# Layer norms of a two-layer encoder step: variance and scale on whole rows instead of token columns and diagonals

## The chip, the cores and the metric

The kernel runs on one core of one Trainium2 chip. The metric is the device time of one execution in microseconds, from runs of the whole program. The engines are named as the profile names them: PE (TensorE, matrix products), PEld (its weight loads), DVE (VectorE), ACT (ScalarE), POOL (GpSimd) and SP (SyncE, which issues the DMAs). Each engine takes its instructions in the order in which the program was written; a wait on a semaphore holds up all that stands behind it on that engine.

## The reference

One inference step of an encoder with two layers, on 576 tokens (512 of a new prompt and 64 of a running stream) of 1024 features. Layer 0 mixes with an mLSTM and a retention in parallel, layer 1 with multi-head latent attention. After each mixer and after each SwiGLU feed-forward network (FFN) stands a residual addition and a layer norm:

```python
def layer_norm(x, g, b):
    mu = mean(x); var = mean(square(x - mu))
    return (x - mu) * rsqrt(var + LN_EPS) * g + b

for layer in range(2):
    m = mixer_ab(x, ...) if layer % 2 == 0 else mixer_c(x, ...)      # each ends in "@ w_out"
    x = layer_norm(ALPHA * x + m, ln_mix_g[layer], ln_mix_b[layer])
    x = layer_norm(ALPHA * x + (silu(x @ w_g) * (x @ w_u)) @ w_down, ln_ffn_g[layer], ln_ffn_b[layer])

def mixer_c(x, ...):
    cq, ckv, kr = split(x @ w_in, (512, 256, 64))
    cq, ckv = rms_norm(cq, g_q), rms_norm(ckv, g_kv)
    q = cq @ w_uq; k, v = ckv_all @ w_ukv      # 8 heads, 128 + 64 rotary columns
    o = softmax(mask(q k^T)) v                 # block-causal, chunks of 64
    return o @ w_out, ckv, rope(kr)
```

All inputs and outputs are float32.

## The kernel before

The activations lie with features on the 128 partitions and tokens along the free dimension: `Z` holds eight feature tiles m = 0 to 7 of 576 tokens. A float32 product is made from a rounded high and a low part of each operand (`Xh`, `Xl`, and for a weight tile `raw` the pair of tiles `r` that ACT casts at line 364 and DVE splits at line 362), three passes of PE for each product. A weight is split shortly before PE uses it.

The tokens are worked in two halves, 288 and 288 around a mixer's output and 320 and 256 around an FFN. So there are eight layer norms: after the mixer of layer 0 (number 0), after its FFN (1), after the attention (2) and after the last FFN (3), each for half 0 and half 1. While half 0 is being normed, PE works on half 1's last output tiles; while half 1 is being normed, PE begins the next stage with half 0.

The steps of one norm are these. For each feature tile m PE leaves the product in a PSUM bank of the pool `mm`, which has three banks, and DVE adds it to the residual in `Z` (the feed, `ln_feed`, lines 1185 and 1187). That addition is also what frees the bank: the tile three places later in the ring can't begin until it is done. `ln_sums` adds the tile to a running sum `s1` (line 1226, DVE), squares it on ACT (line 1223) and adds the square to `s2` (line 1233, DVE). After m = 7 `ln_finish` reduces `s1` and `s2` over the partitions on PE, works out the variance and its inverse root, and then goes over the tiles: `mean` (line 1265, DVE) subtracts the mean, `scaled` (line 1279, DVE) multiplies by gain and inverse root, ACT adds the bias and rounds (lines 1311 and 1318, `Xh` and `Z`), POOL (line 1319) or DVE (line 1314) makes `Xl`. The PSUM banks of these reductions come from a second pool, `x`, with four banks; a single further bank, `o`, collects an attention head's output.

Before the change the inverse root is worked on token columns: PE turns each 128 tokens of `s1` and `s2` into a column by a product with the constant `cvec`, DVE makes ten small operations on 128x3 numbers (lines 1254 to 1256 and `rsqrt`, 539 to 543), puts the three columns on the diagonals of three 128x128 tiles (line 1261), and PE multiplies these by `ones`, which spreads the roots over a row again in the bank R.

The order of the work is written out by hand. Long steps are generators; `spawn` sets one to go on at a later time of a clock that counts PE's modelled time, and `tick`, called between products, lets the due ones run. The pauses are the table `LAG`: `l1` ahead of `ln_finish`, and `l2` in its middle, between the small operations and the scaling of the tiles. What comes due later is written later into each engine's queue.

Behind norm 1 stands the attention's input projection. For its queries (`cq`, two 512-column products of tokens, then a key/value product `kv` of 320 columns) a norm of its own is made for each block of 128 tokens (`norm`, lines 1730 on ACT and 1731 to 1733 on DVE, again with `rsqrt`). In the attention a head's first block, the sample's 64 tokens, has a second accumulator in columns 64 to 128 of the bank `o`; ACT copies the first (line 2021) and DVE adds it (line 2022), the bank addition.

Of the kernel before, what the change touches and what calls it, by code (L numbers as in the profile page):

```python
# [217 lines left out]
class Kern:  # L218
# [335 lines left out]
    def setup(self):  # L554
# [359 lines left out]
    def retention(self):  # L914
# [16 lines left out]
        def s2(i):  # L931
# [30 lines left out]
            ve, hv, tt, rs = (self.smalls(4) for _ in range(4))  # L962
# [68 lines left out]
    def mlstm(self, h, done):  # L1031
# [43 lines left out]
        def s3(half):  # L1075
            ts = HTILES[half]
            n, i0 = len(ts), ts[0]
            den, rc, ve, hv, tt, rs = (self.smalls(n) for _ in range(6))
# [16 lines left out]
            self.rsqrt(rs, ve, hv, tt)  # L1095
# [119 lines left out]
    def ln_sums(self, s, m):  # L1215
        nc = self.nc
        z = self.zt(s.half, m, s.cut)
        if m == 0:
# [7 lines left out]
        nc.vector.tensor_tensor(s.s1, s.first if m == 1 else s.s1, z, ALU.add)
# [9 lines left out]
    def ln_finish(self, s):  # L1236
# [3 lines left out]
        sl = [(0, 128, 0), (128, 256, 0)]  # L1240
        if n > 256:
            sl.append((n - 128, n, 384 - n))
        J = len(sl)
# [9 lines left out]
        dl, vv, hv, tt, rs = (self.smalls(J) for _ in range(5))  # L1253
        V.tensor_copy(dl, x3[:, 0, :, 0])
# [30 lines left out]
        if tail:  # L1285
            A.copy(s.s2, R[:, 0:n])
            A.copy(s.cb, xd[:, 0:n])
            for m in (6, 7):
                z = self.zt(s.half, m, s.cut)
                G.tensor_tensor(z, z, s.cb, ALU.subtract)  # L1290
                G.tensor_tensor(z, z, s.s2, ALU.mult)
            zs = [scaled(m) for m in range(3)]
# [2 lines left out]
            V.tensor_scalar(zs[4], zs[4], bias(4), None, ALU.add)
# [376 lines left out]
    def layer1(self):  # L1672
# [54 lines left out]
        def norm(i, ps, n, g, y):  # L1727
            L = TLEN[i]
            ss, ve, hv, tt, rs = (self.smalls(1)[0:L] for _ in range(5))
            A.activation(y[0:L, 0:n], ps[0:L, 0:n], AF.Square, accum_out=ss)  # L1730
            V.tensor_scalar(ve, ss, 1.0 / n, RMS_EPS, ALU.mult, ALU.add)
# [224 lines left out]
        def attn(h):  # L1956
# [48 lines left out]
            def sc(i):  # L2005
# [7 lines left out]
                if i == 0:  # L2013
# [8 lines left out]
                    V.tensor_tensor(x[:, 64:128], x[:, 64:128], tmp, ALU.add)
# [240 lines left out]
```

## Time and profile before

| | us |
|---|---|
| three runs | 1393.73, 1391.89, 1393.08 (median 1393.08) |
| the profiled execution, its own time | 1393.54 |
| its span, first to last instruction | 1391.6 |
| PE busy | 1351.7 (97%), 9759 instructions |
| DVE busy | 979.5 (70%), 2277 |
| ACT busy | 610.8 (44%), 1295 |
| POOL busy | 155.0 (11%), 182 |
| mean granted TensorE clock | 0.992 |

All the rows below come from one profiled execution of this kernel. A row of the timeline has a group's start, its length until the last of it ended, the engine, the line, the operation, output and inputs, the shape, how many there are, and in brackets the idle time of the engine just ahead with what ended it. A row of the waits has the total, how often, and the longest.

### The profile page before, as it was taken

Reading aid. Unit: us, or ns where it says so; the run is one execution under the profiler, and the core shown is the slowest. Engines: PE = TensorE matmul, PEld = TensorE weight load, DVE = VectorE, ACT = ScalarE, POOL = GpSimd, SP = SyncE. Lnnn points to the kernel's source line nnn. Section 1 sums busy time; section 2 is a strip of 40 time slices with the busy share of each in tenths; the row PEclk is TensorE's granted clock in tenths of the full one; section 3 lists DMA queues with packets and bytes.
Section 4 is the critical chain, followed back from the end, with each engine's and each line's share of the span. In section 5 each row is a group of like instructions: output and inputs, shape, how many; then the busy total and the mean of one; then the engine's idle time right before and its main releaser. Section 6 shows DMA issues by size and latency. Waiting matters only on the chain.

```text
span 1391.6 us, 24628 instructions
## 1 busy us (share of the span) xinstructions
PE 1351.7 (97%) x9759; PEld 1305.6 (94%) x9759; DVE 979.5 (70%) x2277; ACT 610.8 (44%) x1295; POOL 155.0 (11%) x182
## 2 busy tenths in 40 slices
PE   8999999999999999999999999999999999999995
PEld 6778999999999999999987899999999999999995
DVE  6757677678873685588898565667888358647876
ACT  4422333445551453255354466543555235425533
POOL 1100001115000000000021533311320000000000
PEclk9999999999999999999999999999999999999997
DMA  6121122611232123223321000021213312222221
GB/s 218 61 61 55 47 75 59 194 60 61 88 108 79 62 103 109 76 92 95 117 86 59 31 31 31 32 92 44 94 61 108 106 61 92 91 91 77 93 75 68
DMA packets 38234, 112.91 MB, mean 81 GB/s; under 512 B 5024, under 2 KB 12512, under 8 KB 38120
## 3 DMA queue, kind: packets, MB, share of 16 engines
q1 hardware_dynamic: 38120, 111.35, 24.3%
q8 instruction: 76, 1.25, 0.4%
q14 instruction: 38, 0.31, 0.1%
HBM read 107.45 MB, written 3.89 MB: 80 GB/s over the span
## 4 chain that ended last, share of the span: by engine, by line
PE 83%; DVE 10%; ACT 3%; DMA 2%; issue 2%; POOL 0%; SPq 0%; POOLq 0%; ACTq 0%; DVEq 0%
PE mm L465 44%; PE x L465 36%; PE x L533 2%; DVE r L362 2%; DVE Z L1279 1%; DMA raw<-in_w 1%; DVE Z L1265 1%; PE o L465 1%; ACT Xh L1311 1%; DMA Z<-in_x 1%; ACT r L364 0%; ACT Z L1318 0%; DVE small L542 0%; DVE small L541 0%; DVE small L543 0%
## 5 line engine op out<-in xcount | busy, mean ns | idle before, releaser
L465 PE MATMUL mm<-H,r 128*128 128x320 f32 (+2 forms) x2832 | 387.6, 297 | 0.0
L465 PEld LDWEIGHTS mm<-H,r 128*128 128x128 f32 x2832 | 378.3, 189 | 0.3
L465 PE MATMUL x<-Xh,r 128*128 128x288 f32 x1216 | 244.7, 296 | 0.0
L465 PE MATMUL mm<-Xh,r 128*128 128x288 f32 (+2 forms) x1152 | 229.2, 297 | 6.4 <-DVE Z L1185 2.8
L364 ACT CAST r<-raw 128x512 fp32r<-128x512 f32 (+2 forms) x292 | 178.0, 646 | 104.6 <-PE mm L465 76.0
L362 DVE TENSOR_TENSOR r<-raw,r 128x512 fp32r<-128x512 f32 (+2 forms) x276 | 194.4, 733 | 38.0 <-ACT r L364 37.8
L465 PE MATMUL x<-r,r 128*128 128x288 f32 (+2 forms) x1534 | 211.7, 293 | 0.2 <-DVE r L1055 0.2
L465 PEld LDWEIGHTS x<-r,r 128*128 128x128 f32 x1534 | 205.9, 188 | 0.5 <-DVE r L1055 0.5
L465 PEld LDWEIGHTS x<-Xh,r 128*128 128x128 f32 x1216 | 194.6, 188 | 0.5
L465 PEld LDWEIGHTS mm<-Xh,r 128*128 128x128 f32 x1152 | 183.4, 189 | 7.7 <-ACT Z L1318 3.8
L465 PE MATMUL x<-Xl,r 128*128 128x288 f32 x608 | 179.5, 295 | 0.0
L465 PE MATMUL mm<-Xl,r 128*128 128x288 f32 (+2 forms) x576 | 167.1, 298 | 0.0
L364 ACT CAST r<-T 128x512 fp32r<-128x512 f32 (+1 forms) x114 | 86.9, 762 | 127.5 <-DVE T L397 112.0
L465 PEld LDWEIGHTS x<-Xl,r 128*128 128x128 f32 x608 | 114.1, 188 | 0.0
L362 DVE TENSOR_TENSOR r<-T,r 128x512 fp32r<-128x512 f32 (+1 forms) x114 | 96.3, 866 | 18.6 <-ACT r L364 18.6
L465 PEld LDWEIGHTS mm<-Xl,r 128*128 128x128 f32 x576 | 107.2, 189 | 0.1
L465 PE MATMUL mm<-r,Xh 128*128 128x512 f32 (+1 forms) x320 | 98.8, 391 | 4.6 <-DVE r L699 2.6
L1319 POOL TENSOR_TENSOR Xl<-Z,Xh 128x288 fp32r<-128x288 f32 (+2 forms) x36 | 30.7, 853 | 467.0 <-ACT Z L1318 466.5
L465 PEld LDWEIGHTS mm<-r,Xh 128*128 128x128 f32 x320 | 58.8, 192 | 17.9 <-issue 3.0
L1223 ACT ACTIVATE T<-Z 128x288 f32<-128x288 f32 (+2 forms) x56 | 24.8, 443 | 91.8 <-DVE Z L1185 47.4
L465 PE MATMUL mm<-r,Xl 128*128 128x512 f32 (+1 forms) x160 | 61.3, 383 | 0.0
L1580 DVE TENSOR_TENSOR T<-T,x 128x288 f32<-128x288 f32 x38 | 17.2, 453 | 59.1 <-PE x L465 59.1
(316 smaller groups left out, 1725.9 us busy)
## 6 DMA issues: line engine op xcount, KB each, us to landing
raw<-in_w SPq DMA_DIRECT2D x169, 512.0 KB, 3.5
r<-in_w SPq DMA_DIRECT2D x20, 512.0 KB, 3.4
Z<-in_x SPq DMA_DIRECT2D x1, 1280.0 KB
o_y<-Z SPq DMA_DIRECT2D x2, 640.0 KB, 3.3
Z<-in_x SPq DMA_DIRECT2D x2, 512.0 KB, 7.2
Z<-in_x SPq DMA_DIRECT2D x1, 1024.0 KB, 8.7
o_y<-Z SPq DMA_DIRECT2D x4, 256.0 KB, 2.1
Z<-in_x SPq DMA_DIRECT2D x3, 320.0 KB, 4.9
```

The source lines that it names most:

```text
L362: self.lo_engine.tensor_tensor(t[:, 1], src, t[:, 0].bitcast(F32), ALU.subtract)
L364: self.nc.scalar.copy(t[:, 0], src)
L465: self.nc.tensor.matmul(out, lhsT, rhs, start=start, stop=stop, skip_group_check=more)
L533: self.nc.tensor.transpose(out, in_, self.ident[0:n, 0:n])
L1223: nc.scalar.activation(q, z, AF.Square)
L1265: V.tensor_tensor(z, z, xd[:, 0:n], ALU.subtract)
L1279: V.scalar_tensor_tensor(z, z, gain(m), R[:, 0:n], ALU.mult, ALU.mult)
L1311: A.activation(self.Xh[:, a:b], z, AF.Identity, bias=bias(m))
L1319: G.tensor_tensor(self.Xl[:, a:b], z, self.Xh[:, a:b].bitcast(F32), ALU.subtract)
L1580: V.tensor_tensor(s[:, 0:n], s[:, 0:n], ps, ALU.add)
```

## The change

It has four parts.

1. The norm's middle. The `cvec` products, the small operations on token columns, the diagonals and the later `ones` products are gone. PE makes two full-row products, `ones` with `s1` into the bank `xd` (the mean in every partition) and `ones` with `s2` into R; ACT squares `xd`; DVE works out variance and inverse root on whole rows of 288, 320 or 256 numbers, with `rsqrt` writing its last result into R.
2. The pause `l2` is 1.5 for all eight norms (3 to 7 before).
3. The tail, norm 3 of half 1: the last additions to `s1` and `s2` are left out, and PE adds tile 7 and its square to the two banks by two more products. The order of the last tiles among DVE, POOL and ACT is a new one.
4. In the attention, the bank addition of the sample's block moves from right behind its own products to just ahead of the rounding that reads the bank.

```diff
 LAG = {...
-       "l200": 4.5, "l201": 4.5, "l210": 3, "l211": 7, "l220": 3, "l221": 3, "l230": 4.5, "l231": 4.5, "lc2": 0.3,
+       "l200": 1.5, "l201": 1.5, "l210": 1.5, "l211": 1.5, "l220": 1.5, "l221": 1.5, "l230": 1.5, "l231": 1.5, "lc2": 0.3,
...
-    def rsqrt(self, y, v, hv, t):
+    def rsqrt(self, y, v, out, t):
         V.tensor_scalar(y.bitcast(I32), v.bitcast(I32), -0.5, float(0x5F1FFFF9), ALU.mult, ALU.add)
-        for a, b in ((-0.703952253, 0.703952253 * 2.38924456), (-0.50000016, 1.50000048)):
+        for a, b, to in ((-0.703952253, 0.703952253 * 2.38924456, y), (-0.50000016, 1.50000048, out)):
             V.tensor_tensor(t, y, y, ALU.mult)
             V.scalar_tensor_tensor(t, t, a, v, ALU.mult, ALU.mult)
-            V.scalar_tensor_tensor(y, t, b, y, ALU.add, ALU.mult)
+            V.scalar_tensor_tensor(to, t, b, y, ALU.add, ALU.mult)
... ln_sums
+        if m == 7 and s.last and s.half:
+            return
         nc.vector.tensor_tensor(s.s1, s.first if m == 1 else s.s1, z, ALU.add)
... ln_finish
-        for q, src in enumerate((s.s1, s.s2)):
-            for j, (a, b, _) in enumerate(sl):
-                self.mm(x3[:, q, j, :], src[:, a:b], self.cvec[:, 0:2], True, True)
-            if q == 0:
-                self.mm(xd[:, 0:n], self.ones, s.s1, True, True)
-        V.tensor_copy(dl, x3[:, 0, :, 0])
-        V.scalar_tensor_tensor(vv, dl, -1.0, dl, ALU.mult, ALU.mult)
-        V.scalar_tensor_tensor(vv, x3[:, 1, :, 0], LN_EPS, vv, ALU.add, ALU.add)
-        self.rsqrt(rs, vv, hv, tt)
-        for j in range(J):
-            V.tensor_scalar(d, self.ident, rs[:, j:j + 1], 1024.0, ALU.mult, ALU.mult)
+        self.mm(xd[:, 0:n], self.ones, s.s1, True, not tail)
+        if not tail:
+            self.mm(R[:, 0:n], self.ones, s.s2, True, True)
+        else:
+            self.mm(R[:, 0:n], self.ones, s.s2, True, False)
+            self.mm(xd[:, 0:n], self.ones, self.zt(s.half, 7, s.cut), False, True)
+            self.mm(R[:, 0:n], self.ones, s.q, False, True)
+        t, v, y = R[:, 0:n], s.cb, s.s1
...
-        for m in range(lnv if tail else 2):
-            mean(m)
+        A.activation(v, xd[:, 0:n], AF.Square)
+        mean(0)
+        if tail:
+            c = self.tmp("h", n)
+            A.copy(c, xd[:, 0:n])
+            for m in (6, 7, 5):
+                G.tensor_tensor(z, z, c, ALU.subtract)
+        V.scalar_tensor_tensor(v, t, LN_EPS, v, ALU.add, ALU.subtract)
+        self.rsqrt(y, v, t, t)
+        mean(1)
         yield LAG[f"l2{s.which}{s.half}"]
-        R = self.xbank()
-        for (a, b, c), d in zip(sl, dg):
-            self.mm(R[:, a + c:b], self.ones, d[:, c:128], True, True)
... the tail
-            A.copy(s.cb, xd[:, 0:n])
             for m in (6, 7):
-                G.tensor_tensor(z, z, s.cb, ALU.subtract)
                 G.tensor_tensor(z, z, s.s2, ALU.mult)
-            zs = [scaled(m) for m in range(3)]
...
+            for m in range(6):
+                if m in (2, 3, 4):
+                    mean(m)
+                z = scaled(m)
+                if m in (1, 3):
+                    V.tensor_scalar(z, z, bias(m), None, ALU.add)
-            for m in (0, 6, 7, 2, 3, 5):
+            for m in (0, 2, 6, 4, 5, 7):
... the attention
-                    tmp = self.smalls(64)
-                    A.copy(tmp, x[:, 0:64])
-                    V.tensor_tensor(x[:, 64:128], x[:, 64:128], tmp, ALU.add)
                     return
...
+                    if not half:
+                        tmp = self.smalls(64)
+                        A.copy(tmp, x[:, 0:64])
+                        V.tensor_tensor(x[:, 64:128], x[:, 64:128], tmp, ALU.add)
                     split(self.Xh[:, a:b], self.Xl[:, a:b], x[:, c:c + b - a])
```

The other callers of `rsqrt` give their result as `out` and work as before. In the changed file the lines have other numbers: the feed is at 1176 and 1178, `mean` at 1247, `scaled` at 1267, `Xl` at 1302, the norm of the queries at 1719 to 1721, the bank addition at 2029.

The shorter pause moves instructions in DVE's queue. The first place is norm 1, half 0. Here `mm_7121` (before) and `mm_7101` (after) are the banks with half 1's tile m = 4. Before, on DVE:

```order
L1265 TENSOR_TENSOR Z_69<-Z_69,x_7072 128x320
L1279 SCALAR_TENSOR_TENSOR Z_69<-Z_69,lnv_79,x_7134 128x320
L1265 TENSOR_TENSOR Z_69<-Z_69,x_7072 128x320
L1279 SCALAR_TENSOR_TENSOR Z_69<-Z_69,lnv_79,x_7134 128x320
L1187 TENSOR_TENSOR Z_69<-Z_69,mm_7121 128x256
L1233 TENSOR_TENSOR T_3_71<-T_3_71,T_2_70 128x256
L1226 TENSOR_TENSOR T_3_71<-T_3_71,Z_69 128x256
L1265 TENSOR_TENSOR Z_69<-Z_69,x_7072 128x320
L1279 SCALAR_TENSOR_TENSOR Z_69<-Z_69,lnv_79,x_7134 128x320
```

Four of the eight scalings stood behind the feed of m = 4. After, on DVE, from the sixth scaling on:

```order
L1267 SCALAR_TENSOR_TENSOR Z_69<-Z_69,lnv_78,x_7043 128x320
L1247 TENSOR_TENSOR Z_69<-Z_69,x_7042 128x320
L1267 SCALAR_TENSOR_TENSOR Z_69<-Z_69,lnv_78,x_7043 128x320
L1247 TENSOR_TENSOR Z_69<-Z_69,x_7042 128x320
L1267 SCALAR_TENSOR_TENSOR Z_69<-Z_69,lnv_78,x_7043 128x320
L1178 TENSOR_TENSOR Z_69<-Z_69,mm_7101 128x256
L1226 TENSOR_TENSOR T_3_71<-T_3_71,T_2_70 128x256
L1219 TENSOR_TENSOR T_3_71<-T_3_71,Z_69 128x256
```

Now all eight stand ahead of it. In norm 0 the order changes in the same way, there with two more pairs of weight splits of line 362 between.

The second place is norm 1, half 1, in the queue of DVE beside the projection of the queries; `r_389`, `r_392` (before) and `r_389`, `r_394` (after) are split weights of the key/value product. Before:

```order
L362 TENSOR_TENSOR r_389_6753<-raw_417_7243,r_389_6753 128x320
L362 TENSOR_TENSOR r_392_6787<-raw_417_7243,r_392_6787 128x320
L1731 TENSOR_SCALAR small_75<-small_75 128x1
L539 TENSOR_SCALAR small_75<-small_75 128x1
L541 TENSOR_TENSOR small_75<-small_75 128x1
L542 SCALAR_TENSOR_TENSOR small_75<-small_75 128x1
L543 SCALAR_TENSOR_TENSOR small_75<-small_75 128x1
L541 TENSOR_TENSOR small_75<-small_75 128x1
L542 SCALAR_TENSOR_TENSOR small_75<-small_75 128x1
L543 SCALAR_TENSOR_TENSOR small_75<-small_75 128x1
L1733 SCALAR_TENSOR_TENSOR T_2_70<-mm_7277,small_75,T_2_70 128x512
L362 TENSOR_TENSOR r_392_6787<-raw_417_7243,r_392_6787 128x320
```

After it stood two more splits, two more norms of this kind and only then the eight scalings of half 1. Now, behind the first five splits:

```order
L1267 SCALAR_TENSOR_TENSOR Z_69<-Z_69,lnv_78,x_7270 128x256 x2
L1247 TENSOR_TENSOR Z_69<-Z_69,x_7269 128x256
L1267 SCALAR_TENSOR_TENSOR Z_69<-Z_69,lnv_78,x_7270 128x256
L1247 TENSOR_TENSOR Z_69<-Z_69,x_7269 128x256
L1267 SCALAR_TENSOR_TENSOR Z_69<-Z_69,lnv_78,x_7270 128x256
L1719 TENSOR_SCALAR small_75<-small_75 128x1
L539 TENSOR_SCALAR small_75<-small_75 128x1
L541 TENSOR_TENSOR small_75<-small_75 128x1
```

Four scalings stand ahead of the first of the queries' norms and of the three last splits, and the other four ahead of the second norm. ACT's queue moves with it: four `Xh` of line 1299 stand ahead of the square sum of that norm (line 1718) and of the three casts.

The third place is the attention's first head on DVE (`o_8200` and `o_8149` are the bank o, line 1902 or 1890 prepares keys). Before:

```order
L1984 TENSOR_SCALAR T_2_70<-T_2_70,small_75 128x512
L1902 SCALAR_TENSOR_TENSOR T_434_7596<-mm_8147,T_434_7596 128x256
L2022 TENSOR_TENSOR o_8200<-o_8200,small_75 128x64
L1938 SCALAR_TENSOR_TENSOR T_434_7596<-x_8209,T_434_7596 64x320
L1938 SCALAR_TENSOR_TENSOR T_434_7596<-x_8215,T_434_7596 64x256
L1898 TENSOR_TENSOR Xl_73<-o_8200,Xh_72 128x320
```

After:

```order
L1972 TENSOR_SCALAR T_2_70<-T_2_70,small_75 128x512
L1890 SCALAR_TENSOR_TENSOR T_429_7545<-mm_8096,T_429_7545 128x256
L1926 SCALAR_TENSOR_TENSOR T_429_7545<-x_8156,T_429_7545 64x320
L1926 SCALAR_TENSOR_TENSOR T_429_7545<-x_8162,T_429_7545 64x256
L2029 TENSOR_TENSOR o_8149<-o_8149,small_75 128x64
L1886 TENSOR_TENSOR Xl_73<-o_8149,Xh_72 128x320
```

The addition now stands right ahead of the operation that reads its result, behind all of the head's products into the bank.

More of the change, by code (lines that the diff above doesn't have):

```diff
@@ L961, in s2 @@
             mv = self.smalls(8).rearrange("p (h c) -> p h c", h=4)
-            ve, hv, tt, rs = (self.smalls(4) for _ in range(4))
+            ve, tt, rs = (self.smalls(4) for _ in range(3))
             for h in range(4):
@@ L1077, in s3 @@
             n, i0 = len(ts), ts[0]
-            den, rc, ve, hv, tt, rs = (self.smalls(n) for _ in range(6))
+            den, rc, ve, tt, rs = (self.smalls(n) for _ in range(5))
             bs = self.smalls(6 * n).rearrange("p (i c) -> p i c", i=n)
@@ L1239, in ln_finish @@
         n = s.n
[L1240 to L1243, printed above, removed]
         tail = s.last and s.half
-        lnv = 6 if tail else KT
-        x, xd = self.xbank(), self.xbank()
-        x3 = x[:, 0:4 * J].rearrange("p (q j c) -> p q j c", q=2, j=J)
-        for q, src in enumerate((s.s1, s.s2)):
-            for j, (a, b, _) in enumerate(sl):
-                self.mm(x3[:, q, j, :], src[:, a:b], self.cvec[:, 0:2], True, True)
-            if q == 0:
-                self.mm(xd[:, 0:n], self.ones, s.s1, True, True)
-        dl, vv, hv, tt, rs = (self.smalls(J) for _ in range(5))
-        V.tensor_copy(dl, x3[:, 0, :, 0])
-        V.scalar_tensor_tensor(vv, dl, -1.0, dl, ALU.mult, ALU.mult)
-        V.scalar_tensor_tensor(vv, x3[:, 1, :, 0], LN_EPS, vv, ALU.add, ALU.add)
-        self.rsqrt(rs, vv, hv, tt)
-        dg = []
-        for j in range(J):
-            d = self.diag()
-            V.tensor_scalar(d, self.ident, rs[:, j:j + 1], 1024.0, ALU.mult, ALU.mult)
-            dg.append(d)
+        xd, R = self.xbank(), self.xbank()
+        self.mm(xd[:, 0:n], self.ones, s.s1, True, not tail)
[6 more added lines that the diff above has]
+        t, v, y = R[:, 0:n], s.cb, s.s1
         def mean(m):
@@ L1265, in mean @@
             V.tensor_tensor(z, z, xd[:, 0:n], ALU.subtract)
-        for m in range(lnv if tail else 2):
-            mean(m)
+        A.activation(v, xd[:, 0:n], AF.Square)
[4 more added lines that the diff above has]
+            for m in (6, 7, 5):
+                z = self.zt(s.half, m, s.cut)
+                G.tensor_tensor(z, z, c, ALU.subtract)
+        V.scalar_tensor_tensor(v, t, LN_EPS, v, ALU.add, ALU.subtract)
+        self.rsqrt(y, v, t, t)
+        mean(1)
         yield LAG[f"l2{s.which}{s.half}"]
-        R = self.xbank()
-        for (a, b, c), d in zip(sl, dg):
-            self.mm(R[:, a + c:b], self.ones, d[:, c:128], True, True)
         w = s.which
@@ L1286, in ln_finish @@
             A.copy(s.s2, R[:, 0:n])
-            A.copy(s.cb, xd[:, 0:n])
             for m in (6, 7):
                 z = self.zt(s.half, m, s.cut)
-                G.tensor_tensor(z, z, s.cb, ALU.subtract)
                 G.tensor_tensor(z, z, s.s2, ALU.mult)
-            zs = [scaled(m) for m in range(3)]
-            V.tensor_scalar(zs[1], zs[1], bias(1), None, ALU.add)
-            zs += [scaled(m) for m in range(3, 6)]
-            V.tensor_scalar(zs[4], zs[4], bias(4), None, ALU.add)
-            for m in (0, 6, 7, 2, 3, 5):
+            for m in range(6):
[5 more added lines that the diff above has]
+            for m in (0, 2, 6, 4, 5, 7):
                 z = self.zt(s.half, m, s.cut)
                 A.activation(z, z, AF.Identity, bias=bias(m), scale=gain(m) if m > 5 else 1.0)
-                if m in (0, 7, 3, 5):
+                if m in (0, 2, 5, 7):
                     store(m - m % 2, m - m % 2 + 1)
@@ L1728, in norm @@
             L = TLEN[i]
-            ss, ve, hv, tt, rs = (self.smalls(1)[0:L] for _ in range(5))
+            ss, ve, tt, rs = (self.smalls(1)[0:L] for _ in range(4))
             A.activation(y[0:L, 0:n], ps[0:L, 0:n], AF.Square, accum_out=ss)
             V.tensor_scalar(ve, ss, 1.0 / n, RMS_EPS, ALU.mult, ALU.add)
-            self.rsqrt(rs, ve, hv, tt)
+            self.rsqrt(rs, ve, rs, tt)
             V.scalar_tensor_tensor(y[0:L, 0:n], ps[0:L, 0:n], rs, g[0:L], ALU.mult, ALU.mult)
```

12 lines of the change are left out of this document (2 added, 10 removed).

## The prediction

> **What bounds the kernel now.** I read the page's busy times first, then PE's waits by what ended them, and then the timeline around each norm.
>
> ```profile
> PE 1351.7 (97%) x9759; PEld 1305.6 (94%) x9759; DVE 979.5 (70%) x2277; ACT 610.8 (44%) x1295; POOL 155.0 (11%) x182
> PE o L465 <- DVE o L2022: 3.9, 5, 1.1
> ```
>
> PE works 97% of the span, so a microsecond taken off PE counts wherever PE isn't already waiting. The largest sum of waits by cause is the bank addition that the change moves (3.9 in five waits, the longest 1.1). Nearly all of the other waits that the change can touch lie at the norms, and the rows below show DVE or ACT ending them. So two questions decide: does PE still wait at the norms, and is DVE's queue later or earlier there?
>
> **Part 1, PE's own work.** At norm 0, half 0:
>
> ```profile
> 287.99 0.72 PE L465 MATMUL x<-cvec,T 128*128 128x2 f32 x6
> 288.57 0.73 PE L465 MATMUL x<-T,ones 128*128 128x288 f32 x2
> 289.14 0.73 PE L465 MATMUL x<-cvec,T 128*128 128x2 f32 x6
> 296.14 0.75 PE L465 MATMUL x<-T,ones 128*128 128x128 f32 x6
> 309.11 2.37 PE L465 MATMUL mm<-Xh,r 128*128 128x288 f32 x16 [2.66 <-ACT Z L1318]
> 334.01 0.53 PE L465 MATMUL mm<-Xh,r 128*128 128x288 f32 x2 [0.82 <-ACT Xh L1311]
> ```
>
> From start to start the full row costs 0.57 and each set of columns about 0.58; the spreading of the roots takes another 0.59. The change leaves two full rows, 1.14 in place of 2.33, so PE is relieved of 1.19 a norm, some 7 us over all eight, with less for the narrower ones. But in both halves PE waits afterwards (2.66 and 0.82): there the saving only lengthens the wait, unless what PE waits for comes earlier too.
>
> **Part 1, DVE's chain.** The same norm on DVE, and three rows of ACT:
>
> ```profile
> 289.90 0.16 DVE L1254 COPY small<-x 128x3 f32<-128x3 f32 x1 [0.52 <-PE x L465]
> 292.48 0.81 DVE L1265 TENSOR_TENSOR Z<-Z,x 128x288 f32<-128x288 f32 x2
> 294.74 2.50 DVE L362 TENSOR_TENSOR r<-raw,r 128x512 fp32r<-128x512 f32 x4 [0.34 <-ACT r L364]
> 297.16 0.45 DVE L1185 SCALAR_TENSOR_TENSOR Z<-Z,mm 128x288 f32<-128x288 f32 x1
> 299.11 0.45 DVE L1265 TENSOR_TENSOR Z<-Z,x 128x288 f32<-128x288 f32 x1
> 299.59 0.52 DVE L1279 SCALAR_TENSOR_TENSOR Z<-Z,lnv,x 128x288 f32<-128x288 f32 x1
> 308.52 0.45 DVE L1185 SCALAR_TENSOR_TENSOR Z<-Z,mm 128x288 f32<-128x288 f32 x1
> 294.10 2.17 ACT L364 CAST r<-raw 128x512 fp32r<-128x512 f32 x4
> 308.45 0.54 ACT L1318 ACTIVATE Z<-Z,lnv 128x288 f32<-128x288 f32 x1
> 309.45 0.54 ACT L1318 ACTIVATE Z<-Z,lnv 128x288 f32<-128x288 f32 x1
> ```
>
> From the copy to the end of the second mean it takes 3.4 (289.90 to 293.29). A full-row operation that needs the one before costs 0.48 (299.11 to 299.59). The new middle has eight such steps and two means of about 0.4: 4.6, and ahead of it one square on ACT. No row shows these operations at full width in this place; I take 0.48, the nearest row; the ends are 0.40 (the pair of means is 0.81) and 0.55. The chain is 1.2 longer, but starts 0.25 earlier, since it needs one product and a square of 0.45 instead of three sets. So DVE is about 1.0 later at each norm, in exchange for no round trip over PE.
>
> **Part 2, the shorter pause.** This is where I expect the time to go. Half 1's tile m = 7 uses the bank of m = 4, and may not start until DVE has fed m = 4. Before, that feed stood amid the scalings (297.16). Now it stands behind all eight. In norm 0: second mean at 294.25, feed of m = 3 (three operations, 1.1) to 295.35, four scalings 2.75 to 298.1; then four splits, for which ACT casts (2.17) only after its four pairs of `Xh` and `Z`, 1.0 each (308.45 to 309.45), so to 302.0 and the last split to 302.6; four more pairs 3.65 to 306.25; the feed to 306.6. PE, which before took 3.23 a tile (five tiles and the spreading from 289.72 to 306.45), is ready for m = 7 at 302.05. It waits 4.6 and ends m = 7 at 309.85. The next stage's first product needs m = 5's bank, behind two more splits: 309.95, against 309.11. With POOL running beside it DVE's adds get slower; I take +1.2, between +0.8 and +2.3. Half 1 then depends on DVE for its last `Xh` as before (the 0.82), PE's saving disappears in that wait: 0, between -1.2 and +0.5.
>
> Norm 1, half 0, with tiles of 320:
>
> ```profile
> 691.76 0.74 PE L465 MATMUL x<-cvec,T 128*128 128x2 f32 x6
> 693.57 4.15 PE L465 MATMUL mm<-H,r 128*128 128x256 f32 x33
> 707.85 0.70 PE L465 MATMUL mm<-r,Xh 128*128 128x512 f32 x2 [0.95 <-ACT Z L1318]
> 701.26 0.41 DVE L1187 TENSOR_TENSOR Z<-Z,mm 128x256 f32<-128x256 f32 x1
> 706.83 0.55 DVE L1279 SCALAR_TENSOR_TENSOR Z<-Z,lnv,x 128x320 f32<-128x320 f32 x1
> ```
>
> Sums end at 693.0, square 693.4, ten operations of 0.4 to 0.51 to 698.3, feed of m = 3 to 699.3, two scalings 1.0, six pairs of 0.98: the feed of m = 4 ends at 706.55 in place of 701.67. PE's tiles take 2.55 (five and the spreading of 0.59 from 693.57 to 706.90), so it is ready for m = 7 at 703.2, waits 3.4 and ends at 709.15: +1.3 against 707.85.
>
> Norm 1, half 1, beside the queries' projection:
>
> ```profile
> 718.07 1.70 DVE L362 TENSOR_TENSOR r<-raw,r 128x320 fp32r<-128x320 f32 x4
> 719.68 0.15 DVE L1731 TENSOR_SCALAR small<-small 128x1 f32<-128x1 f32 x1
> 721.22 0.75 DVE L1733 SCALAR_TENSOR_TENSOR T<-mm,small,T 128x512 f32<-128x512 f32 x1
> 721.88 1.28 DVE L362 TENSOR_TENSOR r<-raw,r 128x320 fp32r<-128x320 f32 x3
> 727.95 0.86 DVE L1279 SCALAR_TENSOR_TENSOR Z<-Z,lnv,x 128x256 f32<-128x256 f32 x2
> 720.53 0.46 PE L465 MATMUL mm<-r,Xh 128*128 128x320 f32 x2
> 724.41 2.12 PE L465 MATMUL mm<-r,H 128*128 128x512 f32 x8
> 728.67 0.45 PE L465 MATMUL mm<-r,Xh 128*128 128x320 f32 x2
> 734.43 2.62 PE L465 MATMUL x<-r,H 128*128 128x320 f32 x16 [1.64 <-DVE Z L1265]
> 740.52 0.43 PE L533 MATMUL x<-ident,T 64*128 64x64 f32 x4 [0.35 <-DVE T L1733]
> ```
>
> Before, splits and queries' norms (719.68, 721.22) come first, and the scalings at 727.95. Now: PE's sums from 714.8 to 715.85 (1.3 late), DVE's ten operations of 0.43 to 720.0, four splits to 721.6, four scalings 2.5 to 724.1, on ACT the fourth `Xh` and the square sum (1.2) to 725.3, the queries' norm 2.2 to 727.5, and then the sixth split at 727.95. PE reaches that key/value weight (720.53 and five of 0.44, all shifted to 721.5) at 723.7 and waits 4.2. Two splits, four scalings with their `Xl` and the second norm follow: 737.0. PE's next key/value block needs the bank that this norm frees. It began at 728.67 and would be ready at 733.55; it waits 3.5. So it is 8.3 late. The old wait of 1.64 for the last mean and that of 0.35 behind it are gone, leaving +6.3, of which 1.3 came with it: +5.1, between +3 (if ACT and DVE hurry by half of the second wait and more) and +6.5.
>
> Norm 2 has PE waits on weights and feeds already, and the same two relief terms: 0, between -1.2 and +1.
>
> **Part 3, the tail.**
>
> ```profile
> 1375.60 0.88 PE L465 MATMUL x<-cvec,T 128*128 128x2 f32 x4 [2.14 <-DVE T L1226]
> 1376.35 1.20 PE L465 MATMUL x<-T,ones 128*128 128x256 f32 x2
> 1385.20 0.38 DVE L1295 TENSOR_SCALAR Z<-Z,lnv 128x256 f32<-128x256 f32 x1
> ```
>
> A 256-column row costs 1.0 here (1376.35 to 1377.34), so three products behind the last square give `xd` at 1378.1 and R at 1379.1. Square and mean to 1379.0, eight steps of 0.43 to 1382.6, copy 0.4, then about 4.3 of scalings: 1387.3 against 1385.58. On ACT, which ends last, the new order regains most: +1.0, between 0 and +1.7.
>
> **Part 4, the bank addition.** Its 3.9 of PE waits goes: the new place has all products of the head ahead, and the next use of the bank is a head away. What is queued behind it on DVE is a split that reads the bank anyway. With it may go a slow stretch:
>
> ```profile
> 795.50:798.90 3.40, 2.26 (x19) 1.91 (x17) 2.36 (x8) 1.86 (x6) 1.24 (x1) 1.00 0.00 0
> 798.90:802.30 3.40, 3.40 (x17) 3.36 (x16) 1.28 (x4) 1.68 (x4) 1.28 (x1) 0.50 0.00 0
> 306.00:309.40 3.40, 0.74 (x6) 0.54 (x5) 3.29 (x9) 3.30 (x7) 1.93 (x3) 1.00 0.42 147
> 309.40:312.80 3.40, 3.40 (x28) 3.40 (x27) 3.37 (x6) 2.36 (x6) 1.54 (x2) 1.00 0.02 5
> ```
>
> In these windows (span, PE, PEld, DVE, ACT, POOL, granted clock) the stretch with the first 1.14 wait is followed by 3.4 at half clock, 17 matmuls where 30 follow; that is up to 1.7 lost. I take -0.8 of it, so -4.7 with the waits.
>
> But the 2.66 wait at 306.45 brought no half clock. My new waits of 4.6, 3.4, 4.2 and 3.5 are longer. Each could cost 0 to 1.7, and part of that would vanish in a later wait: I take +2.0 in all, between 0 and 6.8. The Trainium skill (TensorE: Matmul & The Clock Gate, Part 1) says that the clock drops to half after an idle free-running window of about 3.4 us. By it the first wait and probably the others are each followed by such a stretch, which is the third rival below. The trace agrees as far as 2.66 staying harmless, and disagrees at 798.9, where 1.14 idle sufficed.
>
> **The sum.** +1.2 + 0 + 1.3 + 5.1 + 0 + 1.0 - 4.7 + 2.0 = +5.9 on the execution's 1393.54, which is 0.46 above the median of the runs: 1399.4 there, 1399.0 beside 1393.08. A measurement tells about 0.2%, 2.8 us, from no change.
>
> **Rivals.**
> - PE's relief counts and the feeds come in time: the whole-row steps run faster than 0.48, or PE arrives later than I say. It decides where the feed of m = 4 ends before 703.2 (norm 1) and the sixth split before 723.7. Then -3.9 - 0.8 and -7 for the products, +1 for the tail: 1382.4. For it speaks that PE is 97% busy; against it that the feed would have to come 3.4 earlier, seven of nine steps' worth. Chance 0.12.
> - The waits come, but the queries' projection loses only some 2 (the squares and casts on ACT overlapping better) and no clock drops: 1393.08 + 1.2 + 1.3 + 2 + 1 - 4.7 = 1393.9. Chance 0.16, within 0.2%.
> - All four waits drop the clock, each by the full 1.7: 1393.08 + 3.9 + 6.8 = 1403.8. Chance 0.17.
> - My forecast, +3 to +10 around 1399.0: 0.55.
>
> The range of my own case is 1396 to 1403. The asked range reaches to 1390, where about a tenth is left below, and 1406 above. Faster 0.12, same 0.16, slower 0.72.
>
> **What would show it.** In the profile after: the waits on `o` gone; PE waiting 3 to 5 us in each half 0 of norms 0 and 1 until a feed (line 1176 or 1178); two waits of 3 to 5 inside the queries' projection, ended by ACT or DVE; the granted clock at half behind some of them. Wrong would be: no PE wait above 2 us between 690 and 745, or steps of lines 541 to 543 at 0.3 or less.

## The result, and the profile after

The changed kernel takes 1400.16 us (median of four runs, 1399.62 to 1400.33), the kernel before 1393.28 in four runs beside it: a ratio of 1.005, with a 95% interval of 1.0033 to 1.0068. It is slower by 6.9 us. The profiled execution took 1400.33, its span is 1398.6, its mean granted clock 0.986 (0.992 before).

The page's busy times after, and PE's waits by what ended them (total, how often, the longest):

```profile
PE 1348.7 (96%) x9647; PEld 1301.9 (93%) x9647; DVE 987.9 (71%) x2236; ACT 612.8 (44%) x1303; POOL 152.8 (11%) x181
```

```profile
PE mm L465 <- DVE Z L1176: 6.8, 4, 5.1
PE mm L465 <- ACT T L1387: 3.4, 1, 3.4
PE mm L465 <- DVE r L362: 3.4, 3, 2.0
PE mm L465 <- DVE Z L1178: 3.2, 1, 3.2
...
PE mm L465 <- ACT r L364: 2.6, 2, 2.4
```

PE has 112 instructions fewer and 3.0 us less busy time, though that time now holds more products at half clock. The waits on `o` are gone. New are a wait of 5.1 for a feed in norm 0 (line 1176), one of 3.4 there for ACT's reading of an FFN bank (1387), one of 3.2 for a feed in norm 1 (1178), and two beside the queries' projection, for a cast (364) and a split (362). The timeline of PE shows them in place:

```profile
305.77 5.56 PE L465 MATMUL mm<-H,r 128*128 128x288 f32 x24 [5.09 <-DVE Z L1176]
317.49 1.13 PE L465 MATMUL x<-T,ones 128*128 128x288 f32 x4
334.70 2.53 PE L465 MATMUL mm<-Xh,r 128*128 128x288 f32 x9 [3.45 <-ACT T L1387]
710.89 4.85 PE L465 MATMUL mm<-H,r 128*128 128x256 f32 x21 [3.20 <-DVE Z L1178]
732.60 0.41 PE L465 MATMUL mm<-r,Xh 128*128 128x320 f32 x1 [2.38 <-ACT r L364]
734.98 0.64 PE L465 MATMUL mm<-r,Xh 128*128 128x320 f32 x1 [1.97 <-DVE r L362]
743.67 0.56 PE L465 MATMUL mm<-r,Xh 128*128 128x320 f32 x2 [0.56 <-DVE small L1719]
```

The row at 317.49 is a norm's new work on PE, about 0.75 to the start of the next product (318.24). The wait at 305.77 is explained by DVE's queue in norm 0, half 0, here the steps of the inverse root, the splits and the end of the scalings:

```profile
289.49 0.47 DVE L541 TENSOR_TENSOR x<-T 128x288 f32<-128x288 f32 x1
289.99 0.47 DVE L542 SCALAR_TENSOR_TENSOR x<-x,T 128x288 f32<-128x288 f32 x1
290.49 0.46 DVE L543 SCALAR_TENSOR_TENSOR T<-x,T 128x288 f32<-128x288 f32 x1
...
299.01 2.69 DVE L362 TENSOR_TENSOR r<-raw,r 128x512 fp32r<-128x512 f32 x4 [2.43 <-ACT r L364]
...
304.84 0.52 DVE L1267 SCALAR_TENSOR_TENSOR Z<-Z,lnv,x 128x288 f32<-128x288 f32 x1
305.27 0.45 DVE L1176 SCALAR_TENSOR_TENSOR Z<-Z,mm 128x288 f32<-128x288 f32 x1
```

A dependent step starts 0.50 after the one before. The feed of m = 4 follows the eighth scaling at once and ends at 305.72, and PE starts then. And behind these waits stands a slow clock (windows: span, then busy time and instructions of PE, PEld, DVE, ACT and POOL, the granted clock, DMA):

```profile
300.40:303.80 3.40, 0.28 (x3) 0.04 (x1) 3.33 (x8) 1.26 (x4) 0.00 (x0) 0.98 0.56 188
303.80:307.20 3.40, 1.43 (x6) 1.43 (x7) 3.19 (x7) 3.30 (x8) 2.90 (x4) 0.50 0.31 120
307.20:310.60 3.40, 3.40 (x16) 3.40 (x16) 2.99 (x7) 1.54 (x4) 0.52 (x1) 0.52 0.22 30
310.60:314.00 3.40, 3.40 (x28) 3.40 (x27) 3.12 (x8) 2.12 (x5) 0.00 (x0) 1.00 0.42 145
334.40:337.80 3.40, 3.10 (x13) 3.10 (x14) 2.79 (x6) 1.44 (x4) 3.40 (x4) 0.50 0.02 5
713.20:716.60 3.40, 3.40 (x15) 3.21 (x15) 3.16 (x6) 1.57 (x4) 2.04 (x3) 0.50 0.00 0
737.10:740.50 3.40, 3.40 (x10) 2.72 (x9) 3.11 (x9) 2.61 (x7) 2.94 (x4) 0.50 0.58 236
798.40:801.80 3.40, 3.40 (x30) 3.36 (x28) 1.28 (x4) 2.27 (x4) 0.00 (x0) 1.00 0.00 0
```

In the third of these windows PE does 16 matmuls where the fourth has 28. The last row is the attention's first head, now at full clock. The trace's clock record has four stretches at half clock between the start and the tail: 6.83 us from 303.67, 3.41 from 334.39, 6.83 from 709.85 and 6.83 from 733.74. Before it had 3.41 at the start (27.5) and 3.41 at 798.9, and both are gone.

Laid side by side, the starts of the same instructions give where the time came from. After is 1.2 ahead on entering norm 0 (this is not the change's doing: the start is the same in both, but this execution has other waits there and not the half clock at 27.5), 0.2 behind at 330.75, just ahead of the wait of 3.45, 4.0 behind when norm 0 is done (offset at line 1397 against 1409, near 340), 4.6 on entering norm 1, 12.3 at the first head, 8.2 at the last, 6.9 on entering norm 2, 5.4 behind it, 5.7 on entering norm 3, and 7.0 at the end of the span. Norms 0 and 1 cost some 13, the attention gives back 5.5, norm 2 another 1.5, norm 3 with the tail takes 1.3.

### The profile page after: what moved, and what is told of

Its sections match the earlier page's. It is cut to its first block, busy times and chain, and to the rows that moved or that the text cites. A ratio compares the mean times of both kernels' runs of the same rounds, so it can differ in the third digit from the quotient of the medians.

```text
span 1398.6 us, 24347 instructions
## 1 busy us (share of the span) xinstructions
PE 1348.7 (96%) x9647; PEld 1301.9 (93%) x9647; DVE 987.9 (71%) x2236; ACT 612.8 (44%) x1303; POOL 152.8 (11%) x181
## 4 chain that ended last, share of the span: by engine, by line
PE 80%; DVE 13%; ACT 3%; DMA 2%; issue 2%; POOL 0%; SPq 0%; ACTq 0%; DVEq 0%; POOLq 0%
PE mm L465 43%; PE x L465 35%; PE x L533 2%; DVE Z L1267 2%; DVE r L362 1%; DVE Z L1247 1%; DMA raw<-in_w 1%; PE o L465 1%; ACT Xh L1299 1%; DVE x L541 1%; DVE x L542 1%; ACT r L364 0%; ACT Z L1306 0%; DMA Z<-in_x 0%; DMA rope<-in_rope 0%
## 5 line engine op out<-in xcount | busy, mean ns | idle before, releaser
L465 PE MATMUL mm<-H,r 128*128 128x320 f32 (+2 forms) x2832 | 392.7, 299 | 8.3 <-DVE Z L1176 5.1
L465 PEld LDWEIGHTS mm<-H,r 128*128 128x128 f32 x2832 | 383.2, 191 | 10.1 <-DVE Z L1176 5.3
```

Source lines behind the costliest of these rows:

```text
L465: self.nc.tensor.matmul(out, lhsT, rhs, start=start, stop=stop, skip_group_check=more)
```

## The experiments

My theory is the prediction's: the time is lost where the shorter pause puts eight scalings ahead of a feed or a split that PE needs, and by the half clock behind those waits; the whole-row arithmetic itself is a small loss, and the bank addition a gain of 4.7. The rivals: the arithmetic on whole rows is the loss and the pause is innocent; the waits cost what they last and the clock nothing. The kernels before that ran beside the four batches took 1393.28, 1393.41, 1393.61 and 1393.02, so below I compare differences to the before of the same chip; the changed kernel's is +6.9.

**The changed kernel with the old pauses.**

```diff
-  "l200": 1.5, "l201": 1.5, "l210": 1.5, "l211": 1.5, "l220": 1.5, "l221": 1.5, "l230": 1.5, "l231": 1.5
+  "l200": 4.5, "l201": 4.5, "l210": 3, "l211": 7, "l220": 3, "l221": 3, "l230": 4.5, "l231": 4.5
```

> The changed kernel with the eight pauses l2 as they were before (3 to 7 in place of 1.5); whole rows, tail and attention as changed. If the shorter pause is what costs (the scalings placed ahead of half 1's feeds and of the queries' norms), the time falls below the kernel before: about -3 us against it, 1388 to 1392, with no PE wait above 3 us in norm 1. If the whole-row arithmetic itself costs (a chain about 1 us longer in each norm), most of the loss stays: 1396 to 1400.

It took 1391.56 (1390.41 to 1394.09), a ratio of 0.9989 (0.9981 to 0.9998): -1.9. So the pauses cost 8.7 of what the change costs. PE's waits in norms 0 and 1:

```profile
308.88 4.18 PE L465 MATMUL mm<-Xh,r 128*128 128x288 f32 x16 [4.72 <-ACT Z L1306]
709.69 0.81 PE L465 MATMUL mm<-r,Xh 128*128 128x512 f32 x2 [2.90 <-ACT Z L1306]
```

These are the waits of before (2.66 and 0.95 on line 1318), both about 2 longer. Counted from the entry into the norm (this run is 1.0 ahead at norm 0, 1.1 behind at norm 1), they end about 0.7 later than before: of 2 us of added wait the larger part is PE arriving earlier. Its relief has gone into the wait, as the prediction said, and DVE's later chain is what is left. But the longer waits have a second price: the clock record has 6.83 us at half clock from 307.36 and 3.41 from 710.13, where the kernel before has none. The three later runs with whole rows and old pauses in norms 0 and 1 have the same two stretches; the two later runs with the old middle and old pauses there have 3.41 in norm 0 and none in norm 1.

**The pause alone**, in the kernel before:

```diff
-  "l200": 4.5, "l201": 4.5, "l210": 3, "l211": 7, "l220": 3, "l221": 3, "l230": 4.5, "l231": 4.5
+  "l200": 1.5, "l201": 1.5, "l210": 1.5, "l211": 1.5, "l220": 1.5, "l221": 1.5, "l230": 1.5, "l231": 1.5
```

> The kernel before with the eight pauses l2 at 1.5 and nothing else changed (columns and diagonals as they were). If the shorter pause costs by its place in DVE's queue, whatever the arithmetic: +4 to +8 us, 1397 to 1401, with the waits of PE in norm 0 half 0 and in the queries' projection. If the longer arithmetic is needed for the loss: within 2 us of before.

1397.92 (1393.9 to 1398.58), a ratio of 1.0027 (1.0018 to 1.0037): +4.5. The pause is a loss without the whole rows too, about half of what it is with them. PE's wait for the feed of m = 4 in norm 0 is 2.97 there (302.10 to 305.08), against 5.09 in the changed kernel (300.68 to 305.77), with the same entry: the whole rows bring PE there 1.4 earlier and the feed 0.7 later.

**The bank addition alone**, in the kernel before:

```diff
-                    tmp = self.smalls(64)
-                    A.copy(tmp, x[:, 0:64])
-                    V.tensor_tensor(x[:, 64:128], x[:, 64:128], tmp, ALU.add)
                     return
...
                     c = 64 * (1 - half)
+                    if not half:
+                        tmp = self.smalls(64)
+                        A.copy(tmp, x[:, 0:64])
+                        V.tensor_tensor(x[:, 64:128], x[:, 64:128], tmp, ALU.add)
                     split(...)
```

> The kernel before with the bank addition of the attention moved and nothing else. The prediction's term: -3.9 us of waits and -0.8 of clock, so -4.7, about 1388.4, between -3.4 and -5.6; the half-clock stretch at 799 us gone. Rival: the wait turns up again at the rounding that reads the bank: 0.

1388.7 (1387.94 to 1390.99), a ratio of 0.9967 (0.9956 to 0.9978): -4.7, the term of the sum.

**The clock.** The changed kernel, with dummy products of 128 columns into a bank that nobody reads, 20 ahead of half 1's m = 7 in norm 0 and 12 in norm 1. They give PE something to do in the two waits for feeds and compute nothing that is used (in the trace each product is two matmuls):

```diff
+    def warm(self, n):
+        o = self.obank()
+        for i in range(n):
+            self.nc.tensor.matmul(o[:, 0:128], self.ones, self.ones, start=True, stop=True, skip_group_check=True)
...
+                if half and m == 7:
+                    self.warm(20)
                 ps = self.bank()
...
+                        if li == 0 and p == 2 and half and m == 7:
+                            self.warm(12)
                         ps = self.bank()
```

> The changed kernel with PE kept busy in two of its new waits: 20 products of 128 columns ahead of half 1's tile 7 in norm 0 (about 4 of the 5.1 us) and 12 in norm 1 (2.4 of the 3.2), into the bank o, which is free there and whose content is not read. If the half clock behind the waits is a good part of the loss, these stretches (303.7 to 310.5 and 709.9 to 716.7) stay at full clock and the time falls by 3 to 5 us, to 1395 to 1397. If DVE alone sets the end there: within 1 us of the changed kernel.

1396.67 (1395.83 to 1397.68), a ratio of 1.0025 (1.0015 to 1.0035): +3.3, 3.6 less than without them. Work that only keeps PE busy makes the kernel faster. The waits and their windows there:

```profile
300.38 4.63 PE L1357 MATMUL o<-ones 128*128 128x128 f32 x40
305.63 3.47 PE L465 MATMUL mm<-H,r 128*128 128x288 f32 x24 [0.62 <-DVE Z L1176]
```

```profile
307.20:310.60 3.40, 3.23 (x25) 3.02 (x24) 3.13 (x8) 1.54 (x4) 0.39 (x1) 1.00 0.24 37
333.40:336.80 3.40, 3.40 (x14) 3.40 (x15) 2.48 (x6) 1.20 (x3) 3.40 (x5) 0.51 0.00 0
```

Tile m = 7 starts at 305.63, no earlier than before (305.77), but its 24 matmuls take 3.47 in place of 5.56. The stretches behind the two feeds are gone, 13.7 us of the changed kernel's 23.9 at half clock; those behind the other two places, where nothing was put, remain.

**The old pauses at one place each**, in the changed kernel: norm 1 (both halves), norm 0 (both halves), norm 1 half 1 alone.

```diff
-  "l210": 1.5, "l211": 1.5
+  "l210": 3, "l211": 7
```

> The changed kernel with the old pauses at norm 1 alone (3 and 7 in place of 1.5 and 1.5), all else as changed. By the prediction's sum norm 1 with the queries costs 1.3 + 5.1 = 6.4, so 1400.2 - 6.4 = 1393.8 and about 1 less for the half clock behind its waits: 1392 to 1395. The starts of the tiles in the two traces, before and after, give +7.8 between the entry into norm 1 and the attention, so 1392.4. The rival, that norm 0 carries the greater part, gives 1397 or more.

```diff
-  "l200": 1.5, "l201": 1.5
+  "l200": 4.5, "l201": 4.5
```

> The changed kernel with the old pauses at norm 0 alone (4.5 and 4.5), all else as changed. By the prediction's sum norm 0 costs 1.2 and a quarter to a half of the 2.0 of half clock: 1398 to 1398.5. By the trace after (gaps of 5.09 and 3.45, two stretches of 6.8 and 3.4 at half clock) norm 0 costs about 5: 1395 to 1396.5. If the two norms' costs add up, this gain and that of norm 1 alone together are the 8.6 by which all the old pauses beat the changed kernel.

```diff
-  "l211": 1.5
+  "l211": 7
```

> The changed kernel with the old pause of 7 only at norm 1, half 1, which runs beside the queries' projection. By the prediction's sum this place costs 5.1 of the 6.4 of norm 1: 1394 to 1396. If half 0's wait of 3.2 with its half clock is the greater part, 1397 to 1399. If the queries' norms come no earlier with the old pause, 1400.

They took 1394.66, 1395.71 and 1398.12, with ratios of 1.0008 (0.9999 to 1.0016), 1.0016 (1.0007 to 1.0025) and 1.0031 (1.0019 to 1.0042): +1.1, +2.1 and +4.5. So the short pause costs 5.8 at norm 1, 4.8 at norm 0, and 2.4 at norm 1 half 1 by itself. 5.8 and 4.8 add up to more than the 7.9 to 8.7 that both give together. That is hardly more than the intervals allow (1.2 or more on either side of each figure), and the traces show no overlap: by the starts the old pauses at norm 1 gain 5.2 there whether norm 0 has the old pauses (the run with all of them) or the short ones. How norm 1's 5.8 divides between its halves is open: by the runs the queries have 2.4 of it, but in the traces the old pause at the queries alone already gives 4.0 at the first head, and that at both halves 4.7. That run's profiled execution (1396.5) was its fastest, so its trace doesn't show what the others lost.

**Whole rows in all norms but the tail's, old pauses, bank addition moved.** `ln_rows` is the changed `ln_finish`, `ln_finish` the one before:

```diff
-  s.task = self.spawn(self.ln_finish(s), LAG[f"l1{s.which}{s.half}"])
+  s.task = self.spawn((self.ln_rows if not (s.last and s.half) else self.ln_finish)(s), LAG[f"l1{s.which}{s.half}"])
```

> The kernel before with the bank addition moved and the whole rows in every norm but the tail's, all pauses as before. What is left of the change against the attention's move alone (1388.7) is then the whole-row arithmetic by itself. The kernel with everything of the change but the pauses took 1391.6, 2.9 more. If the tail is what cost that (+1.0 by the prediction, +1.3 by the two traces), this takes 1390 to 1390.5; if the arithmetic costs it, because DVE is about 1.0 later at each norm, 1391 to 1392; if PE's relief of 1.19 a norm counted, 1382 to 1385.

1390.87 (1388.91 to 1392.11), a ratio of 0.998 (0.9971 to 0.999): -2.7, which is 2.0 more than the bank addition alone, just about what the two intervals can tell. So the whole-row arithmetic by itself gains nothing and is probably a loss, though it leaves PE some 6 us less to do. The two traces can't be set against each other for this: this one is the fastest of its runs, that of the bank addition alone the slowest of its own.

**Whole rows and the short pause in norm 2 alone**, bank addition moved:

```diff
-  s.task = self.spawn(self.ln_finish(s), LAG[f"l1{s.which}{s.half}"])
+  s.task = self.spawn((self.ln_rows if s.which == 2 else self.ln_finish)(s), LAG[f"l1{s.which}{s.half}"])
-  "l220": 3, "l221": 3
+  "l220": 1.5, "l221": 1.5
```

> The kernel before with the bank addition moved, and with whole rows and the short pause in norm 2 alone (after the attention, both halves); the other norms as before. The attention's move alone took 1388.7. The prediction took 0 for norm 2, between -1.2 and +1: 1387.5 to 1389.7. The starts of the tiles before and after give -1.5 for norm 2: 1387.2. If the whole-row arithmetic costs what it costs elsewhere (+2.2 over all norms but the tail), 1389 to 1390.

1384.97 (1384.43 to 1385.68), a ratio of 0.9948 (0.9936 to 0.9961): -8.1, below all that was expected, 3.3 better than the bank addition alone and faster than both kernels. PE at norm 2 with the bank addition alone, timeline and windows:

```profile
968.68 2.37 PE L465 MATMUL mm<-Xh,r 128*128 128x288 f32 x16 [0.72 <-DVE Z L1185]
973.42 0.50 PE L465 MATMUL mm<-Xh,r 128*128 128x288 f32 x2 [1.30 <-DVE Z L1185]
978.39 0.83 PE L465 MATMUL x<-cvec,T 128*128 128x2 f32 x6 [1.54 <-DVE T L1226]
```

```profile
979.30:982.70 3.40, 3.40 (x14) 3.11 (x14) 3.04 (x12) 2.25 (x4) 0.00 (x0) 0.50 0.78 239
982.70:986.10 3.40, 3.40 (x16) 3.40 (x15) 2.70 (x11) 0.00 (x0) 0.00 (x0) 0.50 0.14 55
```

And here:

```profile
967.08 2.38 PE L465 MATMUL mm<-Xh,r 128*128 128x288 f32 x16 [0.41 <-DVE Z L1185]
970.96 0.51 PE L465 MATMUL mm<-Xh,r 128*128 128x288 f32 x2 [0.45 <-DVE Z L1185]
975.78 1.24 PE L465 MATMUL x<-T,ones 128*128 128x288 f32 x4 [1.38 <-DVE T L1226]
```

```profile
979.30:982.70 3.40, 3.40 (x27) 3.40 (x27) 3.18 (x7) 0.73 (x2) 0.81 (x1) 1.00 0.36 134
```

Here the three waits are shorter (2.24 in place of 3.56) and the two windows at half clock behind the last of them don't come. The trace of the bank addition alone is the slowest of its six runs, so this pair shows more than the 3.3. The kernel before has no half clock at norm 2 either, and by the starts this run gains 2.0 on it there. The other 1.3 is then probably the clock: the granted clock of the runs is 0.991 to 0.993 with the bank addition alone and 0.993 to 0.995 here.

**The short pause at norms 2 and 3 only**, in the changed kernel (old pauses at norms 0 and 1), and the same with the old tail beside it:

```diff
-  "l200": 1.5, "l201": 1.5, "l210": 1.5, "l211": 1.5
+  "l200": 4.5, "l201": 4.5, "l210": 3, "l211": 7
```

> The changed kernel with the old pauses at norms 0 and 1, the short ones at norm 2 and at norm 3. If the single costs add up (-5.5 for norm 1, -4.5 for norm 0, each measured alone), 1400.2 - 10.0 = 1390.2, which is 1.4 below the changed kernel with all the old pauses (1391.6): so the short pause gains where nothing is queued that PE needs. If it does nothing at norms 2 and 3, 1391.6; if the two norms' costs overlap, up to 1392.

```diff
 (the run with whole rows in all norms but the tail's, and)
-  "l220": 3, "l221": 3, "l230": 4.5
+  "l220": 1.5, "l221": 1.5, "l230": 1.5
```

> As the run with whole rows in all norms but the tail's (1390.9, old pauses), with the short pause at norm 2 and at half 0 of norm 3. 1389.2 if norm 2's short pause gives the 1.5 that the starts of the tiles show; 1390.9 if it gives nothing. Against the run with the changed tail beside it, the difference is the tail: +0.7 to +1.3.

1391.98 (0.9994, 0.9985 to 1.0003) and 1390.98 (0.9986, 0.9977 to 0.9995): -1.0 and -2.0. Neither gained what I expected of norm 2's pause. The traces say why: against the run with the old pauses of the same kind, the starts gain 2.0 and 1.0 over norm 2, and lose 2.0 in both at norm 3, half 0. With the old pause the last two means and scalings stand on DVE behind half 1's last feed (1370.46 in the run with the old tail); with the short one all eight stand ahead of it (1372.01), and two such pairs take 2.0. The wait ahead of the tail's sums, with the old pause at norm 3 (first row) and the short one (second):

```profile
1371.60 0.61 PE L465 MATMUL x<-cvec,T 128*128 128x2 f32 x4 [2.56 <-DVE T L1226]
```

```profile
1373.15 1.01 PE L465 MATMUL x<-cvec,T 128*128 128x2 f32 x4 [4.52 <-DVE T L1226]
```

The difference of the two runs, on one chip, is the tail: +1.0, which the intervals (1.3 on either side) don't tell from nothing.

**Four banks in the pool mm, three in x**, the changed kernel otherwise:

```diff
-  tc.tile_pool(name="pm", bufs=PM, ...)      # 3
-  tc.tile_pool(name="px", bufs=PX, ...)      # 4
+  tc.tile_pool(name="pm", bufs=4, ...)
+  tc.tile_pool(name="px", bufs=3, ...)
```

> The changed kernel with four banks in the pool mm and three in the pool x (four before). Tile m = 7 then uses the bank of m = 3, whose feed stands ahead of the scalings, and no longer waits for that of m = 4. By the prediction's theory DVE's queue is what is late: the wait only moves to the next product that needs m = 4's bank, a tile of 2.5 to 3.2 later, and what PE loses falls by at most that at each of two places, so 1397 to 1400. If the bank itself were the cause, both waits of half 0 go (8.3 and their half clock): 1391 to 1393. If three banks are too few for the pool x, 1401 or more.

1405.57 (1404.05 to 1407.0), a ratio of 1.0096 (1.0082 to 1.011): +12.6. The total only says that three banks are too few for x: by the starts it is 10.2 behind the changed kernel already at 140, and loses some 5 more in the attention; PE's waits for DVE's line 1219 ahead of products into x, 3.0 in the changed kernel, are 7.3 here. But at the norms it says more than I asked. PE's waits there:

```profile
315.63 2.35 PE L465 MATMUL mm<-Xh,r 128*128 128x288 f32 x16 [1.98 <-ACT Z L1306]
...
716.05 0.70 PE L465 MATMUL mm<-r,Xh 128*128 128x512 f32 x2 [0.78 <-DVE Z L1178]
```

With m = 7 no longer tied to m = 4's bank, the wait moves on, as the theory has it, in norm 0 to the next stage's first product, and comes out 3.1 and 2.4 shorter (5.09 and 3.20 in the changed kernel). But norm 0 and norm 1 become 4.7 and 4.9 cheaper each, more than the waits: there is no half clock in norm 0 and 3.4 us of it in norm 1, in place of 10.2 and 13.7. So bank and queue are one cause: the feed is late by the queue, and it hurts by the bank.

## Why the prediction came out right, and where its steps didn't

A chain of the runs splits the +6.9: bank addition -4.7; rows and short pause in norm 2, -3.3; rows in norms 0 and 1 with the old pauses, and rows with the short pause at norm 3 half 0, +6.0; the tail +1.0; the short pauses of norms 0 and 1, +7.9. Each is a difference of medians whose own intervals are 1.2 to 2.4 on either side. In the two traces behind the +6.0, whose ends lie 5.4 apart, 3.0 has come by the first head, 0.9 more in a wait behind norm 2, 0.9 at norm 3 half 0 (the 2.0 of the short pause less what PE is relieved of there) and the rest in the tail. So the whole rows cost norms 0 and 1 about 3, the half clock behind their longer waits included.

- **The feeds of m = 4** were right in time and place. The prediction had the waits at 4.6 and 3.4; they are 5.09 and 3.20, each ended by the feed that it named. Shifted by the offset at that point, its end of the feed in norm 0 (306.6 - 1.2) is 305.4; it was 305.72. The dependent step taken as 0.48 is 0.50 from start to start. One reading was off: in norm 0 the old feed at 297.16 didn't stand amid the scalings, but ahead of all eight, the first of which is at 298.26. So all eight were moved across it, where norm 1 had four of them ahead already.
- **Norm 0, half 1** was taken as 0, because half 1 would depend on the last `Xh` as before. This step failed, and 3.7 of norm 0's 5.2 lie here. The wait of 3.45 is not the old 0.82 grown longer. That one stood ahead of the last two of a tile's products with `Xh`; the new one stands ahead of the first of them. The old start of this tile, on PE, and a reading of an FFN bank by DVE:

```profile
330.88 2.31 PE L465 MATMUL mm<-Xh,r 128*128 128x288 f32 x14
324.01 0.46 DVE L1409 TENSOR_TENSOR T<-T,mm 128x288 f32<-128x288 f32 x1
```

And after (the tile starts at 334.70, shown above):

```profile
334.26 0.39 ACT L1387 ACTIVATE T<-mm 128x288 f32<-128x288 f32 x1
335.10 0.44 DVE L1397 TENSOR_TENSOR T<-T,mm 128x288 f32<-128x288 f32 x1
```

Before, DVE's reading, which frees one of the three banks of `mm`, stood ahead of half 1's scalings; now it stands behind all eight. So the tile gets a bank only when ACT, behind half 1's last `Xh`, has read another one. It is the mechanism of the feeds at one more place. With the old pauses the same product starts without a wait (331.29 in the run with all of them), and the 0.81 ahead of the last two is back. PE's saving did disappear in the wait, but the wait ends 3.8 later than the old start, and a window at half clock stands behind it.

- **The half clock** is the term that was mis-sized: +2.0 for four waits. Four stretches came, but one of them behind norm 0's half 1, where no wait was foretold, and none behind the last of the four waits, which shrank. Three of them last for two windows. In the first of the two PE, still held up by the wait, was busy for only 1.31, 2.38 and 2.17 of 3.41 us; in the window that stayed single it was busy for 3.10. In all PE is busy for 19.2 us at half clock. If everything takes twice as long there, up to 9.6 is lost (an estimate), of which later waits take back a part: of the 5.3 behind the two feeds, filling the waits gave 3.6 back. So in its mechanism the third rival was nearer than the forecast; its price of 6.8 no run measures as a whole.
- **Norm 1 with the queries** was put at 1.3 + 5.1 for pause and rows together. The pause alone costs 5.8 there by the runs. Of the two waits inside the queries' projection the first was there (2.38 and 1.97 on either side of the sixth split, 4.2 foretold), the second was 0.56 in place of 3.5: the prediction's doubt that ACT and DVE make up some of it was the better half. The old wait of 1.64 is gone, as said.
- **Norm 2** was put at 0; it gains 3.3 by the runs, and 1.5 to 2.0 by traces without half clock there. The step that failed is the judgement that waits there would eat the relief. They got shorter instead, and the half clock that some executions have behind them went too.
- **Norm 3, half 0** had no term. The short pause loses 2.0 there, by the mechanism foretold for norms 0 and 1; the prediction didn't carry it to the last place where half 1's feeds follow a half 0 norm.
- **The tail** (+1.0) and **the bank addition** (-4.7) came out to the tenth, closer than the intervals can confirm. The tail's row of 1.0 was read where the kernel before is already at half clock (from 1375.77); the same pair of products takes 0.5 from start to start at 1372.07 in the run with the old tail, so the price holds for that clock alone.

So the sign and the place are right by a sound mechanism. That the total of 1399.0 is as close to 1400.16 as it is, is luck: norm 2 was put 3.3 too high, and norm 0's half 1, the clock and norm 3 together about 4.3 too low.

## What to carry to other kernels

When a step on an in-order engine is pulled forward, list what it now stands ahead of, and find there the one operation that frees a buffer for the bottleneck engine: its lateness is the price, whatever the step itself saved. The same edit can then gain at one place and lose at another (norm 2 against norms 0, 1 and 3 here), so such a change is tried place by place: only the bank addition and norm 2 kept here give 1384.97, 15 us below all of it together. And a wait of PE is not over when it ends; add the windows behind it.

## What the runs showed of the hardware

The half clock begins on a fixed grid. In the changed kernel the four stretches start 9, 119 and 126 times 3.413 us after the first; in all fourteen traces the distances are whole numbers of it. By the Trainium skill (TensorE: Matmul & The Clock Gate, Part 1) the window is free-running and 3413 ns long, and the traces agree. The Trainium skill asks there for an idle window; here one in which PE was busy for 1.47 of its 3.41 us is enough. The prediction leaned on the 2.66 wait of norm 0, which the kernel before got over at full clock. With the bank addition alone moved, nothing has changed up to there, the wait is 2.66 again, and it is followed by half clock. The windows on that run's grid, and then those of the kernel before on its own:

```profile
306.80:310.20 3.40, 1.47 (x11) 1.50 (x12) 3.37 (x7) 3.04 (x7) 2.94 (x4) 1.00 0.15 60
310.20:313.60 3.40, 3.40 (x16) 3.40 (x15) 3.36 (x8) 2.04 (x5) 0.40 (x1) 0.51 0.02 5
```

```profile
307.40:310.80 3.40, 1.69 (x13) 1.72 (x14) 3.36 (x8) 2.90 (x8) 2.95 (x4) 1.00 0.11 45
310.80:314.20 3.40, 3.40 (x28) 3.40 (x27) 3.37 (x8) 2.18 (x5) 0.19 (x1) 1.00 0.13 18
```

The same wait lies a little otherwise on the grid: PE was busy 1.47 of one window in the first and 1.69 in the second. So one trace can't show that a wait is harmless. What the rule for a window is stays open: the stretch at 798.9 before followed a window with PE busy for 2.26, more than the 1.69 that was let pass.
